# Two of four pooling tiles placed earlier in the mixer's order of input tiles

## The chip, the cores and the metric

The kernel runs on one core of a Trainium2 chip. The metric is the device time of one execution in microseconds. Three timed runs of the kernel before took 1097.93, 1100.98 and 1101.15 us (median 1100.98).

## What is computed

One block of a network in float32, for 512 tokens of width 1024: a gated feed-forward sublayer, a hybrid mixer, a second feed-forward sublayer, each behind a normalisation whose shift, scale and gate come from a conditioning vector; a last normalisation ends it. The change is in the mixer:

```
proj = h @ w_in                                   # 512 x (512 pool | 1536 z | 1536 x, 512 B, 512 C | 24 dt)
for gi, w in enumerate((2, 4, 8, 16)):            # pooling groups, 128 channels each
    pooled = mean of the last w tokens - u        # causal, fewer at the start
    y_pool[gi] = (pooled @ w_pool[gi]) * pool_scale
x, B, C = silu(causal_conv4(x, B, C))
y = ssd_chunked(x, dt, A, B, C) + d_skip * x      # 24 heads of 64, state 128, 4 groups
y_ssm = group_rmsnorm(y * silu(z)) * ssm_norm_g
x_out = x_in + gate * (concat(y_pool, y_ssm) @ w_out)
```

## The kernel before

Activations lie with 128 channels on the partitions and the 512 tokens along the free axis, so each 128-channel slice of the projection is one tile: four p (pooling), twelve z, twelve x, four B and four C, and one small tile for dt. Every float32 operand is split into a high and a low part, and each 128 x 128 block of weights costs three matmuls (`mm3`, L376 to L378). A tile of the projection is thus 8 x 3 = 24 matmuls into one PSUM bank, which is then evacuated by the other engines.

Weights stream from HBM in units of 512 KB on SP's queue (L126), are split by ScalarE (high part, L168) and VectorE (low part, L171), and wait in a ring of five. Rows of another weight (`w_ada`) are reduced on VectorE in the background (L549).

z0 to z3 are made before the loop. The loop in `mixer` then walks over ORDER, 33 places, and over the eight outA and five outB tiles of the output projection behind it. The place of a tile is its number n in this walk, from 0. TensorE executes in the order in which the program is written. The other engines and SP are ordered by a planner, which simulates the program with its own durations and takes the earliest written instruction that is ready.

Beside the products, work hangs on due places in a list `plan`: `at(time, f)` puts a function in, and `until(n + f)` is called before each place and before each eighth of a product, and writes down what is due. A tile is evacuated at n + 1 (EVAC): an x, B or C tile by `conv` (on ScalarE L967, on VectorE the three taps L969 and the closing product L973), a z tile by `silu_z` (L982, L983), a p tile by `pool_mix`. Head pair p starts at STARTS[p]: `fetch` (two rows of decay by DMA), at +0.75 `one` (transposes L1032, on ScalarE the decay L1035 and L1037, on VectorE L1044, L1046 and the mask L1048), at +2 `two` (state matmuls L1061, decay matmuls L1065, on VectorE the state steps L1074 and L1077), at +3 `three` (matmuls L1087, VectorE L1088, on GpSimd the addition L473 and the product L1090), at +4 `squares` (ScalarE L528, GpSimd L473). A group of three pairs has its sums over channels at +4.75 of its last pair (matmuls L494, root L479 to L488 on VectorE) and its norm at +6 (matmuls L517, VectorE L1108, split L467 and L469). None of these numbers depends on where a tile stands in ORDER.

`pool_mix` evacuates a p tile twice on ScalarE (L872, scaled by one over the window, and L873) and builds the moving sum on GpSimd by doubling: tile p_i has a window of 2, 4, 8 or 16 tokens and so i + 1 steps of an addition (L877) and a small copy (L878), then a correction of the first tokens (L881) and a subtraction (L882). The first call also loads w_pool (L1158). The averaged tile is kept in a `big` buffer until `pool_out`, whose place is in POOLS: 33 for p3 and p2, 34 for p1, 36 for p0. There one matmul with w_pool (L888), an evacuation (L890) and a split follow. `big` has 49 buffers, `tmp` 9, PSUM 8 banks.

Of the kernel before, what the change touches and what calls it, by code (L numbers as in the profile page):

```python
# [50 lines left out]

LAST_KS = (10, 11, 12, 3, 2, 1, 0, 13, 14, 15)

ORDER = 'd0 B0 C0 x0 x1 x2 B1 z4 C1 x3 z5 x4 x5 B2 z6 C2 x6 z7 x7 x8 z8 z9 B3 C3 x9 z10 x10 x11 z11 p3 p2 p1 p0'
STARTS = (6, 9, 12.0, 13.25, 16.75, 18, 22, 24, 27, 29, 31, 33)
HEAD = 0.0
STAGES = (0, 0.75, 2, 3, 4)
# [225 lines left out]
class Block:  # L283
# [76 lines left out]
    def mixer_order():  # L360

        def tile(name):
            kind, i = name[0], int(name[1:])
            return ("dt", 0) if kind == "d" else ("in", {"p": 0, "z": 4, "x": 16, "B": 28, "C": 32}[kind] + i)

        return ([tile(n) for n in ORDER.split()] + [("outA", m) for m in range(KD)]
                + [("outB", m) for m in range(MLATE)])
# [936 lines left out]
```

## Time and profile before

| | |
|---|---|
| timed runs | 1097.93, 1100.98, 1101.15 us |
| profiled execution, its own time | 1098.18 us |
| its span, first to last instruction | 1096.3 us |
| mean granted TensorE clock | 0.998 of full speed |
| TensorE busy | 1075.5 us |
| VectorE busy | 851.2 us |
| ScalarE busy | 500.6 us |
| GpSimd busy | 116.9 us |
| mixer's loop in the span | about 399 to 713 us, its 512-token products |

The page's columns: an engine's busy time, its share of the span, its number of instructions. A timeline row gives start, duration, engine, line, operation, what is written and read, how many merged, and in brackets how long the engine had idled and what ended that. POOL is GpSimd, DVE VectorE, ACT ScalarE, PE TensorE. A matmul's recorded duration overlaps with the next one's; what a matmul takes is read from the distance of two starts.

### The profile page before, as it was taken

The page shows a single profiled execution, that of the slowest core. Times are in us where ns is not written, and L with a number is a line of the kernel's source. Part 1 is how long each engine was busy: PE and PEld are TensorE (multiplying, and loading weights), DVE is VectorE, ACT ScalarE, POOL GpSimd, SP SyncE. Part 2 cuts the span into 40 slices and gives each one's busy share as a digit, 9 for nine tenths or more (in the row PEclk, how much of TensorE's full clock was granted, in tenths as well). Part 3 has the DMA queues.
Part 4 walks back from the last instruction along what each step waited for, and adds up shares of the span by engine and source line. Part 5 has one row for each costly group of instructions (what it writes and reads, how often), then busy time and mean ns, then how long its engine had stood idle before and what let it go on. Part 6 is the DMA issues. An engine that isn't in the chain of part 4 may idle for free.

```text
span 1096.3 us, 17024 instructions
## 1 busy us (share of the span) xinstructions
PE 1075.5 (98%) x6764; PEld 954.4 (87%) x6764; DVE 851.2 (78%) x1354; ACT 500.6 (46%) x836; POOL 116.9 (11%) x114
## 2 busy tenths in 40 slices
PE   8999999999999999999999999999999999999997
PEld 7888899999899988887888767899899999999997
DVE  7986978888887848989988777764877778777744
ACT  4442444454444544656565552354434434444532
POOL 0000000000001410012312850121000000000011
PEclk9999999999999999999999999999999999999999
DMA  8865334443346405554445335740132233223222
GB/s 326 305 225 175 127 120 135 144 144 126 111 158 204 152 25 167 173 168 138 144 135 182 122 120 173 231 153 20 42 113 86 91 113 107 95 87 101 75 58 78
DMA packets 45955, 149.43 MB, mean 136 GB/s; under 512 B 5276, under 2 KB 8220, under 8 KB 45876
## 3 DMA queue, kind: packets, MB, share of 16 engines
q1 hardware_dynamic: 45876, 148.35, 41.8%
q8 instruction: 53, 0.87, 0.3%
q14 instruction: 26, 0.21, 0.1%
HBM read 146.18 MB, written 2.15 MB: 135 GB/s over the span
## 4 chain that ended last, share of the span: by engine, by line
PE 72%; DVE 14%; DMA 7%; ACT 4%; issue 2%; POOL 1%; SPq 0%; DVEq 0%; ACTq 0%; POOLq 0%
PE ps_mm L377 19%; PE ps_mm L376 19%; PE ps_mm L378 18%; PE ps_t L376 4%; PE ps_t L377 4%; PE ps_t L378 4%; DVE w_lo L171 3%; DVE w_raw L549 2%; DMA w_raw<-in_w_in_dram 2%; ACT w_hi L168 2%; DVE big L969 2%; DMA w_raw<-in_ada_dram 1%; DMA big<-csd 1%; ACT big L1035 1%; DVE big L973 1%
## 5 line engine op out<-in xcount | busy, mean ns | idle before, releaser
L376 PE MATMUL ps_mm<-big,w_hi 128*128 128x512 f32 (+1 forms) x1446 | 494.3, 342 | 0.5 <-DVE tmp L452 0.5
L377 PE MATMUL ps_mm<-big,w_hi 128*128 128x512 f32 (+1 forms) x1446 | 492.5, 341 | 0.4 <-DVE big L836 0.4
L378 PE MATMUL ps_mm<-big,w_lo 128*128 128x512 f32 (+1 forms) x1446 | 490.9, 339 | 0.0
L376 PEld LDWEIGHTS ps_mm<-big,w_hi 128*128 128x128 f32 x1446 | 272.1, 188 | 35.3 <-issue 2.3
L377 PEld LDWEIGHTS ps_mm<-big,w_hi 128*128 128x128 f32 x1446 | 274.0, 190 | 32.2 <-DVE big L836 0.9
L378 PEld LDWEIGHTS ps_mm<-big,w_lo 128*128 128x128 f32 x1446 | 271.6, 188 | 30.8
L168 ACT CAST w_hi<-w_raw 128x1024 fp32r<-128x1024 f32 (+1 forms) x118 | 120.2, 1019 | 250.2 <-issue 92.0
L171 DVE TENSOR_TENSOR w_lo<-w_raw,w_hi 128x1024 fp32r<-128x1024 f32 (+1 forms) x118 | 143.9, 1221 | 43.8 <-ACT w_hi L168 40.8
L168 ACT CAST w_hi<-row 128x1024 fp32r<-128x1024 f32 x124 | 116.6, 940 | 89.3 <-PE ps_t L377 37.9
L171 DVE TENSOR_TENSOR w_lo<-row,w_hi 128x1024 fp32r<-128x1024 f32 x124 | 134.9, 1088 | 22.4 <-ACT w_hi L168 22.4
L603 DVE SCALAR_TENSOR_TENSOR x<-ps_mm,mod,x 128x512 f32<-128x512 f32 (+1 forms) x111 | 74.7, 675 | 78.5 <-PE ps_mm L378 78.5
L376 PE MATMUL ps_t<-big,w_hi 128*128 128x256 f32 (+1 forms) x428 | 126.8, 296 | 1.9 <-DVE tmp L440 1.7
L377 PE MATMUL ps_t<-big,w_hi 128*128 128x256 f32 (+1 forms) x428 | 127.0, 297 | 0.0
L378 PE MATMUL ps_t<-big,w_lo 128*128 128x256 f32 (+1 forms) x428 | 126.6, 296 | 0.0
L473 POOL TENSOR_TENSOR sacc<-sacc,sq 128x256 f32<-128x256 f32 (+1 forms) x30 | 28.5, 951 | 754.2 <-ACT sq L528 443.5
L376 PEld LDWEIGHTS ps_t<-big,w_hi 128*128 128x128 f32 x428 | 80.5, 188 | 6.6 <-DVE tmp L440 3.0
L377 PEld LDWEIGHTS ps_t<-big,w_hi 128*128 128x128 f32 x428 | 81.5, 191 | 3.6
L378 PEld LDWEIGHTS ps_t<-big,w_lo 128*128 128x128 f32 x428 | 80.4, 188 | 2.1
L467 ACT CAST big<-tmp 128x512 fp32r<-128x512 f32 (+1 forms) x82 | 44.1, 546 | 21.5 <-DVE tmp L400 9.6
L469 DVE TENSOR_TENSOR big<-tmp,big 128x512 fp32r<-128x512 f32 (+1 forms) x66 | 41.5, 640 | 8.0 <-ACT big L467 7.6
L969 DVE SCALAR_TENSOR_TENSOR big<-ps_mm,vec,big 128x511 f32<-128x511 f32 (+2 forms) x60 | 44.6, 744 | 1.5 <-ACT big L967 0.8
L135 DVE TENSOR_TENSOR row<-row 128x1024 f32<-128x1024 f32 x31 | 37.9, 1222 | 3.7 <-DMA row<-in_ffn_inQ_dram 3.1
(180 smaller groups left out, 1149.1 us busy)
## 6 DMA issues: line engine op xcount, KB each, us to landing
w_raw<-in_ada_dram SPq DMA_DIRECT2D x56, 512.0 KB, 3.7
row<-in_ffn_inQ_dram SPq DMA_DIRECT2D x31, 768.0 KB, 4.4
w_raw<-in_ffn_out_dram SPq DMA_DIRECT2D x40, 512.0 KB, 3.8
w_raw<-in_w_in_dram SPq DMA_DIRECT2D x32, 512.0 KB, 3.7
row<-in_ada_dram SPq DMA_DIRECT2D x16, 512.0 KB, 6.4
row<-in_ffn_inQ_dram SPq DMA_DIRECT2D x31, 256.0 KB, 4.7
w_raw<-in_ffn_in_dram SPq DMA_DIRECT2D x14, 512.0 KB, 4.5
big<-csd SPq DMA_DIRECT2D x24, 256.0 KB, 4.3
```

The source lines that it names most:

```text
L135: V.tensor_tensor(out=raw[:, 1:4:2], in0=raw[:, 0:3:2], in1=raw[:, 3:4].broadcast_to([P, 2, NT]), op=ALU.add)
L168: nc.scalar.copy(out=h, in_=r)
L171: nc.vector.tensor_tensor(out=l, in0=r, in1=h.bitcast(F32), op=ALU.subtract)
L376: T.matmul(o, lhsT=hi, rhs=ahi[:, s], start=first, stop=False, skip_group_check=again)
L377: T.matmul(o, lhsT=hi, rhs=alo[:, s], start=False, stop=False, skip_group_check=again)
L378: T.matmul(o, lhsT=lo, rhs=ahi[:, s], start=False, stop=last, skip_group_check=again)
L467: self.nc.scalar.copy(out=hi[:, s], in_=src[:, :n])
L469: eng.tensor_tensor(out=lo[:, s], in0=src[:, :n], in1=hi[:, s].bitcast(F32), op=ALU.subtract)
L473: self.nc.gpsimd.tensor_tensor(out=acc, in0=acc, in1=q, op=ALU.add)
L549: return self.nc.vector.tensor_tensor_reduce(out=w, in0=w, in1=self.cb, scale=scale, scalar=bias, op0=ALU.mult, op1=ALU.add, accum_out=out)
L603: self.nc.vector.scalar_tensor_tensor(out=xs, in0=ps[:, :n], scalar=self.mod[:, gate, m:m + 1], in1=xs, op0=ALU.mult, op1=ALU.add)
L969: V.scalar_tensor_tensor(out=acc[:, s:], in0=ps[:, :NT - s], scalar=tap(3 - s), in1=acc[:, s:], op0=ALU.mult, op1=ALU.add)
```

## The change

ORDER is edited and nothing else: p3 goes from place 29 to place 11, behind z5, and p2 from place 30 to place 18, behind x6. The tiles in between come one or two places later. STARTS, POOLS and all other numbers stay.

```diff
-ORDER = 'd0 B0 C0 x0 x1 x2 B1 z4 C1 x3 z5 x4 x5 B2 z6 C2 x6 z7 x7 x8 z8 z9 B3 C3 x9 z10 x10 x11 z11 p3 p2 p1 p0'
+ORDER = 'd0 B0 C0 x0 x1 x2 B1 z4 C1 x3 z5 p3 x4 x5 B2 z6 C2 x6 p2 z7 x7 x8 z8 z9 B3 C3 x9 z10 x10 x11 z11 p1 p0'
```

## Rows read from the trace of the kernel before

**Rows 1.** The page's busy time: engine, us, share of the span, instructions.

```profile
...
PE 1075.5 (98%) x6764; PEld 954.4 (87%) x6764; DVE 851.2 (78%) x1354; ACT 500.6 (46%) x836; POOL 116.9 (11%) x114
...
```

**Rows 2.** TensorE's waits, 400 to 720 us: engine, line, releaser, total, times, longest.

```profile
...
PE ps_mm L494 <- POOL big L473: 2.4, 1, 2.4
PE ps_mm L517 <- DVE root L488: 2.1, 2, 1.1
PE ps_y L1087 <- DVE tmp L1074: 1.7, 2, 1.2
PE ps_y L1087 <- ACT tmp L890: 0.6, 1, 0.6
PE ps_y L1065 <- DVE big L1048: 0.5, 2, 0.3
```

**Rows 3.** Table by stretches of the whole core; its first line names the columns.

```profile
...
core 0: us, PE busy (x) PEld busy (x) DVE busy (x) ACT busy (x) POOL busy (x), PEclk, DMA share, GB/s
473.00:488.00 15.00, 15.00 (x91) 12.66 (x91) 12.88 (x16) 10.00 (x20) 5.10 (x4) 1.00 0.51 133
488.00:518.00 30.00, 29.02 (x161) 23.88 (x158) 28.39 (x53) 18.52 (x38) 7.34 (x5) 1.00 0.49 154
518.00:536.00 18.00, 18.00 (x111) 14.87 (x110) 16.69 (x27) 10.55 (x23) 3.86 (x3) 1.00 0.53 158
...
598.00:637.00 39.00, 36.63 (x206) 29.63 (x204) 28.87 (x44) 18.16 (x39) 29.25 (x30) 1.00 0.43 139
...
```

**Rows 4.** Timeline of TensorE at 516 and 616: start, us, line, operation, count.

```profile
...
516.80 1.13 PE L517 MATMUL ps_mm<-vec,root 128*128 128x128 f32 x8 [0.98 <-DVE root L488]
...
616.07 0.40 PE L377 MATMUL ps_mm<-big,w_hi 128*128 128x512 f32 x1
616.30 0.39 PE L378 MATMUL ps_mm<-big,w_lo 128*128 128x512 f32 x1
619.06 1.05 PE L494 MATMUL ps_mm<-ones,big 128*128 128x1 f32 x8 [2.37 <-POOL big L473]
...
```

**Rows 5.** Timeline of GpSimd, 608 to 627 us; in brackets idle time and releaser.

```profile
...
608.51 1.49 POOL L877 TENSOR_TENSOR tmp<-tmp 128x511 f32<-128x511 f32 x1
609.96 2.25 POOL L1090 TENSOR_TENSOR big<-big 128x512 f32<-128x512 f32 x1
...
616.75 2.25 POOL L473 TENSOR_TENSOR big<-big,sq 128x512 f32<-128x512 f32 x1
...
619.26 1.79 POOL L882 TENSOR_TENSOR big<-tmp,big 128x512 f32<-128x512 f32 x1
621.02 1.03 POOL L877 TENSOR_TENSOR tmp<-tmp 128x511 f32<-128x511 f32 x1
...
625.47 1.31 POOL L882 TENSOR_TENSOR big<-tmp,big 128x512 f32<-128x512 f32 x1
...
```

**Rows 6.** Timeline of ScalarE, 612 to 634 us.

```profile
...
612.24 0.63 ACT L528 ACTIVATE sq<-big 128x512 f32<-128x512 f32 x1 [3.71 <-POOL big L1090]
...
632.81 1.05 ACT L168 CAST w_hi<-w_raw 128x1024 fp32r<-128x1024 f32 x1 [7.75 <-PE ps_t L888]
...
```

**Rows 7.** Timeline of VectorE around group 0's root, 512 to 517 us.

```profile
...
512.27 0.74 DVE L969 SCALAR_TENSOR_TENSOR big<-ps_mm,vec,big 128x511 f32<-128x511 f32 x1
...
514.45 0.74 DVE L969 SCALAR_TENSOR_TENSOR big<-ps_mm,vec,big 128x509 f32<-128x509 f32 x1
...
516.50 0.15 DVE L488 SCALAR_TENSOR_TENSOR root<-root 128x4 f32<-128x4 f32 x1
...
```

**Rows 8.** Timeline of VectorE at the loop's end, 605 to 636 us.

```profile
...
605.32 0.69 DVE L1048 TENSOR_TENSOR big<-big 128x512 f32<-128x512 f32 x1 [0.98 <-ACT big L1037]
...
615.15 1.58 DVE L1048 TENSOR_TENSOR big<-big 128x512 f32<-128x512 f32 x1 [4.08 <-ACT big L1037]
616.66 1.21 DVE L171 TENSOR_TENSOR w_lo<-w_raw,w_hi 128x1024 fp32r<-128x1024 f32 x1
...
618.56 0.74 DVE L1077 SCALAR_TENSOR_TENSOR big<-big,vec,ps_y 128x512 f32<-128x512 f32 x1
...
620.34 0.74 DVE L479 TENSOR_SCALAR root<-root 128x4 int32<-128x4 int32 x1
...
633.89 2.15 DVE L171 TENSOR_TENSOR w_lo<-w_raw,w_hi 128x1024 fp32r<-128x1024 f32 x1 [3.09 <-ACT w_hi L168]
...
```

**Rows 9.** Timeline of VectorE at pair 5's decay.

```profile
...
531.81 1.06 DVE L1048 TENSOR_TENSOR big<-big 128x512 f32<-128x512 f32 x1
...
```

## The prediction, written before the changed kernel was run

> **What bounds the kernel now.** I read the page's table of busy time first. TensorE is busy for 1075.5 us, 98% of the span [rows 1], so the change can win only what TensorE waits. The view of TensorE's waits, cut to the mixer's loop (400 to 720 us), is the second: five entries, together about 7.3 us [rows 2]. The longest is one wait of 2.4 us of the group-sum matmuls (L494) for an addition on GpSimd (L473). The table by stretches is the third: VectorE idles 1.6 us in 488 to 518 us and 1.3 us in 518 to 536, but 10.1 us in 598 to 637, where GpSimd is busy for 29.25 of 39 us [rows 3]. So in the middle of the loop VectorE is nearly full and TensorE still hardly waits; at its end GpSimd is full and TensorE waits.
>
> The timelines show why. The sums of group 2 are due while the tiles p3 and p2 are being averaged on GpSimd. p3's first addition starts at 608.51 and runs ahead of pair 8's product (L1090); ScalarE waits 3.71 us for that product before it can square it; the rest of p3's chain then stands ahead of the addition of those squares (616.75, 2.25 us), and TensorE, which issued its last matmul at 616.30, goes on at 619.06 [rows 4 to 6].
>
> **The change part by part.** A place in the order is one tile's product, 24 matmuls whose starts lie 0.23 us apart [rows 4], about 5.6 us. The products and their number stay, so TensorE's own work is unchanged. Times of pairs, heads, sums and norms are fixed by place number, and so are the places of the four pool products (33, 33, 34, 36). What moves: the averaging of p3 from place 30 to 12 (about 474 us) and of p2 from 31 to 19 (about 526 us), with two evacuations each on ScalarE (L872, L873), and the load of w_pool on SP. The tiles x4 to x6 come one place later, z7 to z11 two. The smallest distance that this leaves, from the evacuation of x10 and x11 to their pairs (29 to 31.75, 30 to 33.75), is 2.75 places or 15 us, so I cost these delays at nothing.
>
> First term: the wait of 2.4 us. From place 28 to 32 nothing but the pairs' own work is then left on GpSimd. Pair 8's product would follow its addition (608.5), its squares would be summed by about 613, and TensorE comes there at 616.5. Between 0 (another engine is late there) and -2.4 I take -2.4, since GpSimd is the engine named and is seen busy with p3 in just this gap [rows 5].
>
> Second term: TensorE's wait of 0.98 us at 516.80 for the last step of group 0's root (L488) [rows 4]. Between the root's short steps VectorE did the three taps of x6's convolution from 512.27 on, 0.74 us each [rows 7]. Behind the change x6 is evacuated a place later. Those 2.2 us leave the gap, and p3's averaging is over by then. I take -1.0; the other bound is +3.8, if p3 makes VectorE late (second rival).
>
> Third term: three waits, 2.3 us in all, of pair 10's last matmuls (L1087) at 638 to 641, for its state steps on VectorE (L1074) [rows 2]. VectorE came to these only behind L171, which ScalarE held up until 633.89 and which then took 2.15 us instead of 1.21, because p1's averaging ran beside it [rows 6, 8]. With GpSimd free sooner, p1's averaging is over by 628, and L171 takes 0.9 less. ScalarE's own wait of 7.75 us for L888 stays, for TensorE's order there is the same [rows 6]. Bounds 0 and -2.3; I take -0.9.
>
> Fourth term, the price. VectorE's instructions get longer beside GpSimd: L1048 1.58 against 0.69 us, L171 2.15 against 1.21, a root step 0.74 against 0.15 for another [rows 7, 8]. Added up over the six instructions of such length and the five root steps from 604 to 636 us that is about 8.6 us of VectorE for some 28 us of GpSimd, 0.31 for 1. p3's chain is ten instructions and 8.1 us, p2's eight and 5.6 us (the first and the last of each: [rows 5]). So 2.5 us of VectorE's time move to about 474 to 486 and 1.7 us to about 526 to 533. In the first stretch one convolution less is on VectorE (2.2 us of taps) and it idles 2.1 of 15 us [rows 3]: hidden. Without this cover it would be late at group 0's root. In the second the nearest thing that TensorE needs is pair 5's masked decay (L1048 at 531.81, already lengthened to 1.06 us), and it waits up to 0.3 us for such a step already [rows 2, 9]. VectorE idles 1.3 us in this stretch [rows 3], so 0.4 us remains. I take +0.4, within 0 and +4.3 (second rival).
>
> The Trainium skill, page "SBUF — State Buffer", section "Who interferes with whom", speaks against the change: a VectorE instruction with two inputs in SBUF and a GpSimd instruction that reads SBUF exclude each other, and the second waits until the first ends. The trace agrees in kind: L1048 and L171, which grew, have both inputs in SBUF, while L1077 between them, which reads PSUM, kept its 0.74 us [rows 8]. By full exclusion a microsecond of averaging could cost VectorE up to one, and the sum would come out near the second rival's.
>
> Smaller ones. The load of w_pool now stands in SP's queue at place 12, among pair 2's rows and a weight load; it is one issue, and no split of a weight is among the things TensorE waits for [rows 2]: nothing, and at most a fraction of a microsecond later rows for pair 2. The buffers held longer are w_pool's and, for 21 and 14 places, the averaged tiles; since the tiles behind them come later by as many places, one more buffer of the 49 is in use at most: nothing, or an SP wait (third rival). On ScalarE two evacuations go and two come: nothing either way.
>
> Sum: -2.4 - 1.0 - 0.9 + 0.4 = -3.9. Against the profiled execution, 1098.18 us (span 1096.3 and 1.9 around it), that is 1094.3. The three timed runs have a median of 1100.98 and a lowest of 1097.93; the mean of all four is 1099.6, and I put the forecast on that: 1095.7.
>
> **The rivals.** *The wait is handed on.* x10 and x11 are evacuated at 29 and 30 instead of 27 and 28, so two convolutions (4.5 us of taps) come onto VectorE between 595 and 615, just where group 2's sums and pairs 9 and 10 are due. For it: nothing is behind them any more but z11, p1 and p0. Against it: VectorE idles 10.1 us in this stretch [rows 3], two of its gaps 0.98 and 4.08 us [rows 8], and loses the slow-down beside GpSimd. If it holds, 2 of the 2.4 us come back as a wait of L494 or L1087 and 0.9 is not won either: -1.0, so 1098.6.
>
> *The price is paid in the full middle; slower.* If VectorE loses a microsecond for each of GpSimd's, p3 costs 8.1, less 2.1 idle and 2.2 of taps: group 0's root comes 3.8 us later, which is not won but lost. p2 costs 5.6, less 1.3: pair 5 is 4.3 us late. With -2.4 and -0.9 the total is +4.8: 1104.4. It decides from about 0.53 for 1, where p3's cover (4.3 of 8.1) is used up. For it: 1.6 us of idle time in 30 [rows 3]. Against it: the 0.31 measured.
>
> *The change does not do what it says.* Only TensorE's order is written out; ScalarE, VectorE, GpSimd and SP are ordered by a planner from its own durations. It may put the averaging elsewhere, or an instruction that waits ahead of one that TensorE needs, as the wait of 7.75 us shows it can [rows 6]. The buffers belong here. That may go either way by 1 to 4 us; I put it at no change, 1099.6.
>
> **How the numbers follow.** Forecast 0.50, handed on 0.24, paid in the middle 0.17, planner 0.09. About 0.3% (3.3 us) is what a measurement of this kernel can tell from no change. The forecast lies beyond it with 0.42, inside with 0.08; the first rival is 0.04 faster, 0.18 same, 0.02 slower; the second 0.03 same, 0.14 slower; the third 0.02, 0.04, 0.03. Together 0.48 faster, 0.33 same, 0.19 slower. The range goes from 1091.5 (all of the third term, -5.3 or somewhat more in total, against the lowest run) to 1101.8, which takes in the first rival on the highest run and leaves the second outside. The forecast's own range is 1092.5 to 1098.
>
> **What would show it.** Right: no wait of L494 for L473 near 616; p3's L877 at about 474 and p2's at about 526; L517 at about 516 without a wait; L171 near 633 at about 1.2 us. Wrong: L1065 or L517 waiting over 1 us for VectorE between 486 and 545 (second rival); L494 or L1087 waiting for VectorE at 612 to 640 (first); the averaging elsewhere, or new waits of SP for a buffer in the middle (third).

## The result and the profile after

The kernel became slower: 1110.5 us (median; 1108.72 to 1111.52) against 1100.28 (1097.93 to 1101.15) for the kernel before, a ratio of 1.0097 [1.0085, 1.0109], or +10.2 us. The forecast, 1095.7, and its range, 1091.5 to 1101.8, both missed; "slower" had been given 0.19. The profiled execution took 1110.1 us, its span 1108.1, with a mean granted clock of 0.992.

The page's line of busy time, the first thing to read, answers to [rows 1]:

```profile
...
PE 1080.7 (98%) x6764; PEld 958.6 (87%) x6764; DVE 850.4 (77%) x1354; ACT 500.3 (45%) x836; POOL 117.4 (11%) x114
...
```

The instructions are the same in number, and VectorE's and GpSimd's work is the same to a microsecond. TensorE is "busy" 5.2 us longer for the same matmuls. TensorE's waits in the loop (columns and cut as in [rows 2]):

```profile
...
PE ps_mm L517 <- DVE root L488: 4.7, 1, 4.7
PE ps_t L1061 <- DVE tmp L1046: 2.8, 3, 1.3
PE ps_y L1087 <- ACT tmp L1068: 2.7, 1, 2.7
PE ps_y L1087 <- DVE tmp L1074: 2.5, 2, 1.7
```

Every wait of [rows 2] that the forecast meant to remove is gone: L494 waits for nothing, group 0's L517 waits for nothing, and so does pair 10's L1087. Four others stand in their place, 12.7 us instead of 7.3. The table by stretches answers to [rows 3], three of its stretches moved along with the work; the last two rows are the places where the granted clock (the column behind POOL's) is below 1:

```profile
...
476.00:491.00 15.00, 13.86 (x72) 11.25 (x70) 8.85 (x8) 9.03 (x19) 12.30 (x14) 1.00 0.44 129
491.00:521.00 30.00, 25.96 (x141) 20.83 (x142) 25.84 (x43) 13.31 (x28) 7.65 (x6) 0.94 0.48 160
...
601.00:640.00 39.00, 36.56 (x205) 29.86 (x203) 31.27 (x54) 20.16 (x42) 12.43 (x9) 1.00 0.50 154
...
513.00:517.00 4.00, 3.25 (x11) 2.71 (x11) 3.85 (x8) 1.55 (x3) 0.00 (x0) 0.57 0.67 213
643.00:647.00 4.00, 3.66 (x22) 3.48 (x24) 1.77 (x4) 0.31 (x2) 1.76 (x4) 0.57 0.44 163
...
```

In 476 to 491 GpSimd is at work for 12.30 us, and ScalarE and VectorE, which had 10.00 and 12.88 of 15 us in [rows 3], now have 9.03 and 8.85: they are not overloaded there, they wait. Twice the clock of TensorE falls to 0.57 in the mean of 4 us, which is 4 x 0.43 = 1.7 us lost each time (taken from single microseconds: 1.70 and 1.71).

That makes a ledger. The loop from the dt product (L1179) to the first product of 256 tokens takes 314.07 us before and 322.60 after, +8.5. Its waits are +5.4 and the clock costs 3.4, together +8.8. So what is to be explained lies in the waits and in what the clock does behind two of them. The rest of the profiled execution took 784.1 before and 787.5 after; over all kernels below it lies between 784.1 and 787.5. Of these 3.4 us, 2.4 lie ahead of the first 512-token products (L847 starts at 18.06 us before and at 20.44 after), where the granted clock was 1.00 before and 0.66 and 0.65 in the means of 10 to 15 and 15 to 20 us after. The change does not reach this stretch, so I assign nothing to it.

By place, the 12.7 + 3.4 us of the changed kernel are: 5.2 + 1.7 at 486 to 517 us, 1.7 at 542, 1.0 at 608, and 4.7 + 1.7 at 638 to 647.

**The first place.** GpSimd's timeline, with p3's first and last step and what stands between them for pair 1:

```profile
...
478.38 1.30 POOL L877 TENSOR_TENSOR tmp<-tmp 128x511 f32<-128x511 f32 x1 [17.16 <-ACT tmp L872]
...
480.89 1.46 POOL L473 TENSOR_TENSOR big<-big,tmp 128x384 f32<-128x384 f32 x1
...
482.44 1.28 POOL L1090 TENSOR_TENSOR big<-big 128x512 f32<-128x512 f32 x1
...
487.18 1.31 POOL L882 TENSOR_TENSOR big<-tmp,big 128x512 f32<-128x512 f32 x1
...
```

ScalarE, which goes through its instructions in the planner's order, has the squares of pair 1 (L528) ahead of pair 2's decay (L1037) and of a convolution's last step (L972):

```profile
...
483.76 0.63 ACT L528 ACTIVATE sq<-big 128x512 f32<-128x512 f32 x1 [2.42 <-POOL big L1090]
484.30 0.61 ACT L1037 ACTIVATE big<-big 128x512 f32<-128x512 f32 x1
...
495.63 0.63 ACT L972 ACTIVATE tmp<-big 128x512 f32<-128x512 f32 x1 [6.77 <-DVE big L969]
...
```

VectorE waits for that decay, and then works through its backlog beside the second half of p3's chain and the work of pair 1 that stands behind it on GpSimd. The second part of the fence is group 2's root, the other place:

```profile
...
484.95 1.80 DVE L1048 TENSOR_TENSOR big<-big 128x512 f32<-128x512 f32 x1 [3.47 <-ACT big L1037]
...
487.27 2.29 DVE L171 TENSOR_TENSOR w_lo<-w_raw,w_hi 128x1024 fp32r<-128x1024 f32 x1
489.49 1.62 DVE L1046 TENSOR_TENSOR tmp<-big,dst 128x384 f32<-128x384 f32 x1
...
493.23 2.30 DVE L969 SCALAR_TENSOR_TENSOR big<-ps_mm,vec,big 128x511 f32<-128x511 f32 x3
...
633.42 0.15 DVE L507 TENSOR_SCALAR root<-ps_mm 128x4 f32<-128x4 f32 x1
...
636.50 1.28 DVE L549 CUSTOM_DVE_ANT_0 w_raw<-w_raw,cb,vec 128x1024 f32<-128x1024 f32 x1
...
640.76 1.19 DVE L486 TENSOR_TENSOR root<-root 128x4 f32<-128x4 f32 x1
...
642.18 1.02 DVE L488 SCALAR_TENSOR_TENSOR root<-root 128x4 f32<-128x4 f32 x1
...
```

The wait goes round: GpSimd makes ScalarE late by 2.42 us, ScalarE makes VectorE idle for 3.47, and VectorE makes ScalarE idle for 6.77. That last wait is also made of longer instructions. From L1048 at 484.95 to the first tap of the convolution at 493.23 VectorE takes 8.28 us for five instructions (L1048, L1044, L171, L1046, L171), which take 4.64 in e4 below, where nothing is averaged on GpSimd. TensorE first waits 1.29 us for L1046 at 491.16; its longest wait, 2.68 us from 509.9 on, comes more than 20 us behind p3's last step, and pair 3's decays on ScalarE stand between. Its timeline (the longest waits in the middle and at the end, and the two products that now don't wait, as answers to [rows 4]):

```profile
...
512.62 0.49 PE L1087 MATMUL ps_y<-big,tmp 128*128 128x128 f32 x2 [2.68 <-ACT tmp L1068]
...
513.86 1.22 PE L1087 MATMUL ps_y<-big,tmp 128*128 128x128 f32 x4 [0.75 <-DVE tmp L1074]
...
526.83 1.05 PE L517 MATMUL ps_mm<-vec,root 128*128 128x128 f32 x8
...
629.52 0.95 PE L494 MATMUL ps_mm<-ones,big 128*128 128x1 f32 x8
...
643.34 2.04 PE L517 MATMUL ps_mm<-vec,root 128*128 128x128 f32 x8 [4.74 <-DVE root L488]
...
```

**The second place.** The sums of group 2 are on time (629.52, no wait). VectorE comes to the root 2.95 us after they end (633.42), because a background reduction (L549), the closing product of z11 (L983) and the pairs' own steps are ahead of it, and x10's and x11's steps ahead of these. It then spreads the ten short root steps over 9.8 us, with L171, L1044, L1046, L1088 and another reduction between them, and takes 0.97 to 1.19 us for four steps of about 0.16, where pair 9's addition and product and p1's averaging run on GpSimd beside them. L517 is late by 4.74 us. Then its eight matmuls take 2.04 us instead of 1.05: the clock is at 0.50.

### The profile page after: what moved, and what is told of

Read it like the earlier page. It is cut to its first block, busy times and chain, and to the rows that moved or that the text cites. A ratio compares the mean times of both kernels' runs of the same rounds, so it can differ in the third digit from the quotient of the medians.

```text
span 1108.1 us, 17022 instructions
## 1 busy us (share of the span) xinstructions
PE 1080.7 (98%) x6764; PEld 958.6 (87%) x6764; DVE 850.4 (77%) x1354; ACT 500.3 (45%) x836; POOL 117.4 (11%) x114
## 4 chain that ended last, share of the span: by engine, by line
PE 75%; DVE 13%; DMA 6%; ACT 3%; issue 2%; POOL 1%; SPq 0%; DVEq 0%; ACTq 0%; POOLq 0%
PE ps_mm L377 19%; PE ps_mm L376 19%; PE ps_mm L378 19%; PE ps_t L376 4%; PE ps_t L377 4%; PE ps_t L378 4%; DVE w_lo L171 3%; DMA w_raw<-in_ada_dram 2%; DMA big<-csd 2%; DVE w_raw L549 2%; DVE big L969 1%; ACT w_hi L168 1%; ACT big L1035 1%; PE ps_mm L494 1%; PE ps_mm L517 1%
## 5 line engine op out<-in xcount | busy, mean ns | idle before, releaser
L171 DVE TENSOR_TENSOR w_lo<-w_raw,w_hi 128x1024 fp32r<-128x1024 f32 (+1 forms) x118 | 145.4, 1233 | 42.2 <-ACT w_hi L168 39.1
L171 DVE TENSOR_TENSOR w_lo<-row,w_hi 128x1024 fp32r<-128x1024 f32 x124 | 134.9, 1088 | 22.4 <-ACT w_hi L168 22.4
L473 POOL TENSOR_TENSOR sacc<-sacc,sq 128x256 f32<-128x256 f32 (+1 forms) x30 | 28.5, 951 | 756.2 <-ACT sq L528 445.5
L469 DVE TENSOR_TENSOR big<-tmp,big 128x512 fp32r<-128x512 f32 (+1 forms) x66 | 42.4, 653 | 8.1 <-ACT big L467 7.7
```

What stands on the lines that cost most here:

```text
L171: nc.vector.tensor_tensor(out=l, in0=r, in1=h.bitcast(F32), op=ALU.subtract)
L469: eng.tensor_tensor(out=lo[:, s], in0=src[:, :n], in1=hi[:, s].bitcast(F32), op=ALU.subtract)
L473: self.nc.gpsimd.tensor_tensor(out=acc, in0=acc, in1=q, op=ALU.add)
```

## The experiments

Each ratio is against the kernel before, run on the same chip. Three columns are from the profiled run of each kernel: the loop; TensorE's waits in it; what a granted clock below 1 cost in it (the sum over microseconds of 1 less the clock). The last is the loop less both.

| kernel | median us | ratio [95%] | loop | waits | clock | rest |
|---|---|---|---|---|---|---|
| before | | | 314.1 | 7.3 | 0 | 306.8 |
| after | 1110.5 | 1.0097 [1.0085, 1.0109] | 322.6 | 12.7 | 3.4 | 306.5 |
| e1_p3_only | 1106.24 | 1.0059 [1.0036, 1.0083] | 321.4 | 10.1 | 5.1 | 306.2 |
| e2_p2_only | 1098.53 | 0.9992 [0.9983, 1.0002] | 312.1 | 4.7 | 1.7 | 305.7 |
| e3_late_avg | 1107.56 | 1.0070 [1.0053, 1.0086] | 320.4 | 12.5 | 3.4 | 304.5 |
| e4_no_avg | 1105.57 | 1.0049 [1.0034, 1.0064] | 320.8 | 9.4 | 6.8 | 304.6 |
| e5_norm7_after | 1099.64 | 1.0009 [0.9999, 1.0018] | 313.4 | 5.2 | 1.7 | 306.5 |
| e7_norm7_p2 | 1094.53 | 0.9970 [0.9959, 0.9981] | 309.2 | 2.7 | 1.7 | 304.8 |
| e8_norm7_before | 1098.14 | 0.9994 [0.9984, 1.0003] | 311.6 | 4.2 | 1.7 | 305.7 |
| e9_avg_behind | 1105.75 | 1.0062 [1.0041, 1.0083] | 316.8 | 8.8 | 1.7 | 306.3 |
| e10_behind_norm7 | 1094.26 | 0.9961 [0.9949, 0.9974] | 308.3 | 2.8 | 0 | 305.5 |
| e11_norm7_g2 | 1106.33 | 1.0084 [1.0060, 1.0108] | 319.3 | 10.3 | 1.7 | 307.3 |
| e12_no_ada_end | 1104.67 | 1.0059 [1.0043, 1.0075] | 317.7 | 9.1 | 1.7 | 306.9 |

The rest stays within 304.5 to 307.3 while the loop goes from 308 to 323 (in e3 and e4 the clock falls 2.9 and 2.0 us before TensorE goes on, so some 1.4 and 1.0 us are counted twice there and the rest is too low by as much). In all thirteen kernels the loop is long by what TensorE waits and by what its clock loses, and by little else.

**e1_p3_only.** Only p3 moves; p2 is back at the end.

```diff
-... z5 p3 x4 x5 B2 z6 C2 x6 p2 z7 ... z11 p1 p0
+... z5 p3 x4 x5 B2 z6 C2 x6 z7 ... z11 p2 p1 p0
```

> p3 stays at place 11, p2 goes back behind p3's old place at the end (z11 p2 p1 p0). Theory A, GpSimd's averaging in the full middle (ScalarE stands in order behind pair products that wait for the averaging, VectorE is slowed beside it): the stalls of TensorE at 486 to 517 us with their half clock, about 8 us in the changed kernel, stay; p2's of 2.3 us near 540 goes: 1106 to 1109 us. Theory B, the tiles behind come later and VectorE is late at the end: the wait for group 2's root (4.9 us and 1.6 at half clock) shrinks to half, the middle is clean: 1102 to 1104 us.

Measured: 1106.24 us (1103.16 to 1108.71), +7.1 against 1099.16. The middle stall is whole (waits of 2.7, 1.6 and 0.7 before 522 us), the wait of 1.7 near 540 too, and a root makes L517 wait 2.4 us. The time is the one of theory A, but the wait near 540, which theory A had going with p2, stays.

**e2_p2_only.** Only p2 moves.

```diff
-... z5 p3 x4 x5 B2 z6 C2 x6 p2 z7 ... z11 p1 p0
+... z5 x4 x5 B2 z6 C2 x6 p2 z7 ... z11 p3 p1 p0
```

> p2 moves ahead behind x6 (place 17), p3 stays at the end (z11 p3 p1 p0). Theory A: p3's stalls at 486 to 517 go, p2's 2.3 us near 540 stay, and the old wait of 2.4 us at group 2's sums comes back: 1101 to 1104 us. Theory B: the wait for group 2's root is about half of the changed kernel's 6.5 us and the old wait comes on top: 1104 to 1107 us.

Measured: 1098.53 us, no change, below both theories. TensorE's waits in this kernel's loop:

```profile
...
PE ps_mm L517 <- DVE root L488: 3.9, 3, 3.0
PE ps_t L1061 <- DVE tmp L1046: 0.8, 1, 0.8
```

The wait of L494 for GpSimd is gone as in the forecast, but one of 3.0 us for a root takes its place at the end, and the clock falls behind it: 7.3 us of waits have become 4.7 and 1.7 of clock. So p3 carries the loss in the middle, and the wait that is handed on at the end comes even with p2 alone.

**e3_late_avg.** The order of after and its evacuations, but the averaging of p3 and p2 is written at places 30 and 31 as before; ScalarE's copies wait in buffers.

```diff
-            d = self.pool_mix(i, ps)
+            u, s = self.pool_mix(i, ps)            # evacuation only
+            def average(): held["d"] = self.pool_avg(i, u, s)
...
+            if i > 1: at({3: 30, 2: 31}[i], average)
```

> The changed order; p3 and p2 are evacuated at their new places, but their averaging on GpSimd is written down at places 30 and 31, where it stood before (the scaled copy is held in a big buffer instead of a tmp). Theory A: the stalls at 486 to 517 and at 540 go, about 10 us; the wait at the end stays or grows by the old 2.4 us: 1100 to 1104 us. Theory B: the tiles are as late as in the changed kernel, so the time stays: 1108 to 1112 us.

Measured: 1107.56 us, between the two theories. The middle stall is gone (0.8 us of waits before 522), so it comes from the averaging and not from the moved product or evacuation. But the time hardly fell, for the end got worse:

```profile
...
PE ps_mm L517 <- DVE root L488: 8.0, 2, 7.6
PE ps_y L1093 <- DVE tmp L1080: 2.3, 2, 1.5
...
PE ps_mm L494 <- POOL big L473: 1.1, 1, 1.1
```

(Lines lie 6 higher in e3, e9 and e10: L1093 is L1087, L1080 is L1074.) With GpSimd as full there as before and VectorE with x10 and x11 later, the root waits 7.6 us. The order at the end is worse than the old one when the averaging is the same.

**e4_no_avg.** In the order of after, p3 and p2 skip the averaging.

```diff
         u, s = self.big(), self.tmp()
...
+        if i > 1:
+            return u
```

> The changed order with the averaging of p3 and p2 left out (their tiles go unaveraged into the pool product; 13.7 us of GpSimd less). Theory A: the stalls of the middle go, only the wait for group 2's root is left: 1099 to 1103 us. Theory B: nothing but the slow-down of VectorE goes: 1106 to 1110 us.

Measured: 1105.57 us, +6.4 on 1099.16. Only part of the loss goes with the averaging; both theories' numbers are missed. The waits (lines lie 2 higher: L1089 is L1087):

```profile
...
PE ps_mm L517 <- DVE root L488: 4.7, 1, 4.7
PE ps_y L1089 <- DVE tmp L1076: 2.5, 2, 1.7
PE ps_y L1089 <- ACT tmp L1070: 1.1, 1, 1.1
PE ps_t L1063 <- DVE tmp L1048: 1.0, 1, 1.0
```

The wait of 2.7 in the middle is gone. The 4.7 us at group 2's root, the 1.7 near 540 and the 1.0 of L1063 are unchanged, without any averaging of p3 and p2. These come with the places of the x and z tiles, not with the averaging of p3 and p2; p1's averaging still runs beside the root here. And the 1.1 + 1.7 us near 535 were followed by a fall of the clock for some 7 us, as the 4.7 at the root were: 3.4 us each time, so 9.4 us of waits cost another 6.8.

**e5_norm7_after, e7_norm7_p2, e8_norm7_before.** All norms one place later, on the order of after, on e2's and on the order before.

```diff
-SUMS, NORM = 4.75, 6
+SUMS, NORM = 4.75, 7
```

> The changed kernel with NORM 7 instead of 6: every group's norm (and TensorE's L517 for it) is written one place, 5.7 us, later behind its sums. Theory: TensorE's wait for group 2's root (4.9 us, and some 1.6 us at half clock behind it) is only a due place too early for a VectorE that has x10, x11 and z11 to do; it goes, and the stalls of the middle stay: 1103 to 1105 us. Rival: VectorE's backlog is what costs, and shows at the next thing due (L1087, L1061): 1108 to 1111 us.

> Only p2 moved ahead, and NORM 7. The waits for roots (3.2 us for group 2, 0.7 and 0.5 for groups 3 and 0 in the run with p2 alone, 1098.5 us) go: 1094 to 1096 us. If VectorE's backlog shows elsewhere: 1098 to 1099 us.

> The kernel before with NORM 7. Its two waits for roots (1.0 and 1.1 us) go, the waits of 2.4 us for GpSimd and 2.3 us for pair 10 stay: 1097 to 1098 us. If the backlog shows elsewhere: no change, 1099 us.

Measured: 1099.64, 1094.53 and 1098.14 us. On the order before it does nothing that can be told (0.9994 [0.9984, 1.0003]); on the order of after it takes back the loss, 1.0097 to 1.0009, more than either theory for e5 had. What is left of e5's waits is the middle stall by itself, as in the changed kernel to the tenth:

```profile
...
PE ps_y L1087 <- ACT tmp L1068: 2.7, 1, 2.7
PE ps_t L1061 <- DVE tmp L1046: 1.7, 2, 1.3
PE ps_y L1087 <- DVE tmp L1074: 0.8, 1, 0.8
```

So the waits at 542, 608 and 638 hang on where the norms stand, and the middle stall doesn't. In e8 pair 10's waits are gone as well, which its expectation had staying, and pair 11 waits 1.7 us instead.

**e9_avg_behind.** As e3, but p3's averaging is written at 13.5 (behind pair 1's product) and p2's at 19.

```diff
-            if i > 1: at({3: 30, 2: 31}[i], average)
+            if i > 1: at({3: 13.5, 2: 19}[i], average)
```

> The changed order, with p3's averaging written at place 13.5, behind pair 1's product and squares (p2's at 19 as in the changed kernel; the scaled copies are held in big buffers). Theory 'head of the line': the stall at 486 to 517 comes from pair 1's product standing behind p3's steps and ScalarE standing in order for its squares; it goes with the same work on GpSimd in the same full stretch: 1101 to 1104 us. Theory 'shared input': it comes from VectorE being slowed beside GpSimd; it stays, a place later: 1107 to 1111 us.

Measured: 1105.75 us (1101.40 to 1107.21), between the two theories; the profiled execution was the lowest, 1101.4. GpSimd does the same chain some 10 us later, counted from pair 1's L1088, and pair 1 goes first. Its timeline:

```profile
...
477.23 1.29 POOL L1096 TENSOR_TENSOR big<-big 128x512 f32<-128x512 f32 x1
...
485.56 1.04 POOL L883 TENSOR_TENSOR tmp<-big 128x511 f32<-128x511 f32 x1
...
492.01 1.30 POOL L888 TENSOR_TENSOR big<-tmp,big 128x512 f32<-128x512 f32 x1
...
```

and ScalarE's and VectorE's (L1054 is L1048 of after, L1052 is L1046):

```profile
...
478.56 0.63 ACT L528 ACTIVATE sq<-big 128x512 f32<-128x512 f32 x1 [0.42 <-POOL big L1096]
...
479.74 1.37 DVE L1054 TENSOR_TENSOR big<-big 128x512 f32<-128x512 f32 x1 [0.67 <-ACT big L1043]
...
481.63 1.21 DVE L171 TENSOR_TENSOR w_lo<-w_raw,w_hi 128x1024 fp32r<-128x1024 f32 x1
482.76 0.55 DVE L1052 TENSOR_TENSOR tmp<-big,dst 128x384 f32<-128x384 f32 x1
...
```

ScalarE waits 0.42 instead of 2.42 us, and TensorE's waits before 522 us are 1.2 instead of 5.2, in the profiled execution with no fall of the clock there. So the place ahead of pair 1's product is what cost. But two things went with it. Counted from pair 1's L1088 (476.97 in after, 474.47 here), VectorE starts the second mask 2.7 us earlier, which is the waiting; and it needs 4.63 instead of 8.28 us from there to the convolution's first tap (484.37), because L171 and L1046 no longer start while GpSimd is at work. Together that is 6.4 us, and no run has one without the other. The wait of 4.7 at group 2's root stays.

**e10_behind_norm7.** e9 with NORM 7, both cures.

> Both remedies on the changed order: p3's averaging at place 13.5 behind pair 1's squares, and NORM 7. If the two stalls (p3's at 486 to 517, group 2's root at the end) are all that the change costs, and its gains are real (no wait for GpSimd at group 2's sums, none at group 0's root), it beats the kernel before: 1092 to 1096 us. If the recovered time shows at other waits: 1097 to 1100 us.

Measured: 1094.26 us (1093.96 to 1094.62), 0.9961 [0.9949, 0.9974]: faster than both kernels, and the one whose runs lie closest together. Two small waits are left, and the clock stays at 1.00:

```profile
...
PE ps_y L1093 <- DVE tmp L1080: 1.9, 2, 1.1
PE ps_y L1093 <- ACT tmp L1074: 0.9, 2, 0.5
```

**e11_norm7_g2.** After, with group 2's norm alone a place later.

```diff
-                at(s + NORM, self.group_norm, g)
+                at(s + NORM + (g == 2), self.group_norm, g)
```

> The changed kernel with only group 2's norm one place later (33 to 34). If the recovery of 10.9 us with NORM 7 is that one due place: 1099 to 1102 us, the wait for pair 4's state steps near 540 staying with its 2.3 us. If the other groups' later norms did it: 1104 to 1110 us.

Measured: 1106.33 us (1104.07 to 1110.76): a miss for the view that group 2's root alone carries the gain of e5. The wait of L517 is gone, but pair 11 now waits:

```profile
...
PE ps_y L1087 <- ACT tmp L1068: 4.1, 2, 2.7
PE ps_y L1087 <- DVE tmp L1074: 3.6, 3, 1.7
```

Of these, 1.42 and 1.12 us lie at 658 and 660 and are new; the 1.7 near 540 stays, and is gone in e5, where group 0's norm is later too. So the gain of NORM 7 is that of several norms, and one wait less was partly handed on.

**e12_no_ada_end.** After, with three background reductions (L549) moved from places 28, 30 and 32 behind the loop.

```diff
-            self.pump({"outA": i // 4, "outB": 2}.get(kind, 0 < n < 9 or n > 9 and n % 2 == 0))
+            self.pump({"outA": i != 3, "outB": 2}.get(kind, 0 < n < 9 or 9 < n < 28 and n % 2 == 0))
```

> The changed kernel, NORM 6, with the three background reductions (L549, 1.28 us of VectorE each) of places 28, 30 and 32 moved to places 33, 34 and 35. Theory, VectorE's backlog from x10, x11 and z11 makes the root late: the wait of 4.9 us shrinks by about as much as leaves VectorE ahead of the root, 2.6 to 3.8 us, and the half clock behind it goes with it: 1104 to 1107 us. Rival, the root is late for its place in the order on VectorE or beside GpSimd, whatever else is queued: 1109 to 1111 us.

Measured: 1104.67 us (1103.17 to 1107.66). VectorE ends the root in time, and L517's wait and the fall of the clock behind it are gone:

```profile
...
632.97 0.15 DVE L488 SCALAR_TENSOR_TENSOR root<-root 128x4 f32<-128x4 f32 x1
...
```

The loop is 4.9 us shorter than in after (4.7 + 1.7 less, and a new wait of 1.1 for L1048). VectorE's load at the end, then, is what makes the root late; the norm's place only decides whether TensorE sees it. The load works in two ways here. With less of it the ten root steps take 3.2 us (629.90 to 633.12) instead of 9.8, each 0.15 to 0.17, because they are done before GpSimd starts pair 9's addition at 633.13. How much a root without lengthened steps, under the same load, would have saved was not tried.

## Why the prediction was wrong

**What held.** TensorE's own work did not change (the rest of the ledger, 306.8 and 306.5). The first two terms came as written: L494's 2.4 us and the wait for group 0's root are gone. p2's price was even below the 0.4 taken: the one wait of TensorE while p2 is averaged (540.74 to 548.4), 1.74 us at 542.15, is there in e1 too (1.75), where p2 isn't averaged there, and e2 shows no loss in the middle. The planner did put the averaging where the order said. The other half of the third rival, "an instruction that waits ahead of one that TensorE needs", did come: the waiting L528 stands ahead of pair 2's decay on ScalarE.

**The third term came by another way, which is luck.** Pair 10's waits are gone (one of the three, 0.6 us, was for ScalarE's L890 in [rows 2], not for VectorE). But the split of [rows 8], L171 at 633.89, is not made shorter ahead of pair 10's state steps. In the changed kernel it stands behind them:

```profile
...
651.46 1.22 DVE L171 TENSOR_TENSOR w_lo<-w_raw,w_hi 128x1024 fp32r<-128x1024 f32 x1
...
```

Here VectorE has done pair 10's L1074 by 650.9, TensorE comes to pair 10's L1087 at 654.0, and ScalarE no longer has the 7.75 us for L888 that the term let stay. In e8, the old order with the norms later, L171 keeps its length and pair 10 does not wait either:

```profile
...
633.61 2.18 DVE L171 TENSOR_TENSOR w_lo<-w_raw,w_hi 128x1024 fp32r<-128x1024 f32 x1 [3.06 <-ACT w_hi L168]
635.72 0.84 DVE L1074 SCALAR_TENSOR_TENSOR tmp<-tmp,dec,ps_t 128x64 f32<-128x64 f32 x4
...
```

What the kernel before has between these two is group 2's norm, three L1108 from 635.97 on and a split (L469), and its first L1074 starts at 638.54.

**The step that failed first: p3 in the fourth term, "In the first stretch ... hidden".** I weighed VectorE's idle time against a slow-down of its instructions, which was only a part of the account. The part that I left out is a wait through three in-order queues: p3's first steps ahead of L473 and L1090 on GpSimd, L528 on ScalarE behind L1090, pair 2's decay behind L528, VectorE behind the decay. Idle time of VectorE in the stretch (2.1 us in [rows 3]) covers nothing when VectorE itself is kept waiting; it idled 3.47 us for one operand. And the wait made the slow-down larger. It moved VectorE's two-input instructions beside the rest of p3's chain and beside the work that came later with it, the sum of pair 1's squares (L473) and L1009. The same thing stood in my own rows: p3 ran ahead of L1090 and ScalarE waited 3.71 us for it [rows 5, 6]. I read it as a fault of the old place; it is how p3's chain and a pair's product meet where both come due, and place 12 has pair 1's. The term priced at 0 measured 5.2 us of waits and 1.7 of clock, against group 0's wait of 0.98 that went. e9 shows that the order is the cause: the same chain behind pair 1, and 4.0 of the 5.2 are gone. It doesn't tell the waiting (2.7 us of VectorE's delay) from the longer instructions (3.65 us).

**The second: "The smallest distance that this leaves ... is 2.75 places or 15 us, so I cost these delays at nothing".** I measured how long each moved tile had until its own pair, and not what VectorE had to do in between for others. x10, x11 and z11, two places later, came onto VectorE in the 10 us before and behind group 2's sums; in 630 to 640 it is busy for all 10.00 us. L494 was no longer held up, and L517 was: 4.7 us, and 1.7 of clock. "The wait is handed on" had the mechanism, but at L494 or L1087 and with 2 us. Some 3.5 of the 9.8 us of root steps are again lengthening beside GpSimd. e4 shows that this loss needs no averaging of p3 and p2 (4.7 us without), e12 that it goes when VectorE has less to do. The same kind of shift may have given the 1.7 near 542, which is argued from the timeline only: a reduction (L549) at 540.37 stands ahead of pair 4's L1074 on VectorE, behind group 0's norm and x6's later convolution.

**The rivals.** I treated "handed on" and "paid in the middle" as alternatives and put "slower" only with the second. They happened together, and at two places: 6.9 us in the middle and 6.4 at the end, 13.3 against 7.3 won. Their sum was never formed, so the range ended below it. The second rival had the wrong places (neither group 0's root nor pair 5 is late) but not a wrong mechanism. The Trainium skill, page "SBUF — State Buffer", section "Who interferes with whom", has a VectorE instruction with two inputs in SBUF and a GpSimd instruction that reads SBUF lock each other out. The trace agrees, instruction by instruction: L171 at 487.27 ends 1.07 us behind GpSimd's L882 (488.49), L1046 at 489.49 ends 0.42 behind L473 (490.69), and the four long root steps end within 0.03 us of the end of the GpSimd instruction that was running when they started. So neither 0.31 nor 1 for 1 is a price of averaging; what it costs depends on which VectorE instructions it meets. In e9 p3's chain meets the end of the taps, which read PSUM, other instructions that read it (L1080, L1083, L1050) and 2.6 us in which VectorE idles; only L979 and L1054 grow there, by 0.9 us together against e4. At group 2's root the lengthening, four steps at 0.97 to 1.19 instead of 0.16, is some 3.5 of the 13.7 us from L494's start to the root's end, against a wait of 4.74; e5 has the same lengthened steps and no wait.

**What the forecast lacked altogether** is the clock: [rows 3] had 1.00 throughout, and I priced a wait at its own length.

**What was won all the same.** With p3's averaging behind pair 1 and the norms a place later (e10), the new order takes 1094.26 us against 1098.14 for the old order with the same norms (e8): 3.9 us, the size of the forecast's sum. These two are from different chips, with the kernel before at 1098.37 and 1098.99. e10 changes the buffers of the copies as well, so I claim the size and not the sum's parts. And p3's move has no share in it that can be told: e7, where only p2 moves and p3 stays at the end, takes 1094.53 us on e8's chip, 0.9970 [0.9959, 0.9981] against e10's 0.9961 [0.9949, 0.9974]. With p2 away, L494's wait for GpSimd is gone already (e2).

**Open.** Why the planner puts pair 3's copy (L1068 at 512.32) behind a convolution's last step on ScalarE was not tried.

## What to carry to other kernels

When a block of work moves ahead on a side engine, look at the first thing of the main chain that comes due behind it on that engine, and then at what stands behind the waiter on the next in-order engine; an engine's idle time covers a delay only if the delay doesn't reach its own operands. Then look which instructions the delay brings side by side on engines that hinder each other. When tiles are put back by two places, add up what the engine that evacuates them has to do ahead of the next deadline of any group, not only the distance to the tile's own use. Rivals that concern different stages can all be true at once, so form their sum as a case of its own.

## What the runs showed that was not expected

A wait of TensorE can cost more than its length. After the 2.68 us without a matmul at 509.9 to 512.6, and after the 4.74 at 638.6, the granted clock was 0.50 (of the levels 2.4 and 1.2 GHz, the lower), as single microseconds of the changed kernel show:

```profile
...
512.00:513.00 1.00, 0.38 (x2) 0.30 (x2) 1.00 (x2) 0.57 (x2) 0.00 (x0) 1.00 0.45 180
...
515.00:516.00 1.00, 1.00 (x4) 0.81 (x3) 1.00 (x2) 0.00 (x0) 0.00 (x0) 0.50 0.95 369
...
517.00:518.00 1.00, 1.00 (x6) 0.83 (x5) 0.90 (x3) 1.00 (x4) 0.03 (x1) 1.00 0.79 274
...
```

The clock is still 1.00 in the microsecond of the wait, falls when TensorE is at work again, and is back within 4 us: 1.7 us lost. In e1, e3 and e4 a fall lasted twice as long and cost 3.4, in e3 and e4 beginning within waits of 7.6 and 4.7 us. The length of a wait alone does not decide: 2.3 us of L494 in e8 was followed by a fall, 2.37 us of the same line in the kernel before [rows 4] was not, and in e4 1.11 and 1.74 us close together were.

It also differs between executions of one kernel, and with it the time. The runs of e11 took 1104.07, 1104.41, 1108.25 and 1110.76 us at mean granted clocks of 0.996, 0.994, 0.991 and 0.988, e9's took 1101.40 at 0.997 and 1105.31 to 1107.21 at 0.991 or 0.992; e10's five all lie within 0.7 us at 0.995 or 0.996. The changed kernel's four had 0.990 to 0.992. So a lower clock in the changed kernel is not a chance of one profile. But the kernel before, too, ran at 0.991 to 0.997 beside these experiments, and its profiled execution at 0.998 was among its best: a fall of the clock that a profile does not show may be there in the next run.
